# Right halves of the sample's output weights split beside the first outputs; one DRAM tensor for a pair's gated values and one for its sums; attention outputs loaded sooner

## The chip, the core and the metric

The kernel runs on one core of a Trainium2 chip. The metric is the device time of one execution in microseconds (us); the median of three runs before the change is 1537.46 us (1533.11 to 1540.15).

The engines are TensorE (PE, with its weight loads, PEld), VectorE (DVE), ScalarE (ACT), GpSimd (POOL) and SyncE (SP). Each executes its own instructions in order; semaphores order them between engines. In this kernel every DMA is issued by SP, in SP's order, and runs on 16 DMA engines.

## The reference

One encoder layer is applied to two batches with the same weights: the prompt (512 rows) and the sample (1024 rows), each row with 1024 columns, in float32.

```python
def _trunk(x, ...):
    h = _rmsnorm(x, norm_attn_g)
    z = h @ w_in                        # q, k, v, and two halves of a convolution's input
    a_out = _window_attn(q, k, v, bias, band, sink)      # 8 heads, |q-k| <= 128
    c = ca * jax.nn.sigmoid(cb)
    c = _dwconv(c, conv_dw_w, conv_dw_b)                 # 31 taps
    c = jax.nn.silu(_layernorm(c, conv_ln_g, conv_ln_b))
    x = x + jnp.concatenate([a_out, c], axis=-1) @ w_out
    h = _rmsnorm(x, norm_ffn_g)
    u = _dwconv(h @ w_up, ffn_dw_w, ffn_dw_b)            # 3 taps, 2 x 2816 columns
    x = x + (jax.nn.silu(u[..., :D_FF]) * u[..., D_FF:]) @ w_down
    return _rmsnorm(x, norm_final_g)
```

## The kernel before

**Precision and tiles.** Every float32 matrix product is made of three products of parts: an operand is rounded to a high part (fp32r) by a cast on ScalarE, and the low part is the operand less the high part, a subtraction on VectorE or GpSimd. `split` (lines 219 to 224) makes both parts; its low part (L223) goes to GpSimd by default and to VectorE with `dve=True`. Matmuls are 128 x 128 by 128 x 512. The 512 rows of the prompt are blocks 0 to 3, the 1024 rows of the sample blocks 4 to 11, of 128 rows each.

**Slots.** SBUF is cut by hand into slots: 15 of class q (4096 bytes a partition), 4 of class c (4224 bytes), 61 of class h (2048 bytes) and some small ones. `sb.tile` takes the free slot of the least class that is big enough, the one that was freed longest ago first; `among` restricts the classes. A slot is given back when the Python object is dropped, and whoever gets it next waits for the instructions that still use it.

**Order.** The program is written as a main line of matmul steps and generators of side work. Each step calls `tick`, which advances the first generator in the queue `side` at a set rate; `drain` runs a queue to its end. The program's order gives priorities; a scheduler that simulates the time of each instruction then orders each engine's instructions. Only in the stages behind the ones described here is TensorE's order written by hand.

**The stages round the change.**

- The prompt's feed-forward up projection runs over 22 column blocks j (`ffn_step`, L933). For a block, `up_half` multiplies the gate's and the value's columns (L329, L330, L332 in `proj`, into the two banks u), ScalarE evacuates a bank (L888), and VectorE adds the other two taps (L884). `gate` (L906) makes the gated value, 128 x 512, and stores it to the DRAM tensor `gt[j]` (L915). The up weights are split on ScalarE and GpSimd (L222, L223).
- Beside it, as side work, `sample` (L947) runs the sample's attention, loads the attention outputs of blocks 4 and 5 back from `catd` (`load_cat`, L703), loads the output weights `w_out` as 16 halves (8 row chunks kc, each with a left and a right half of 512 columns; `load_wo`, L775), splits all 16 (`split_wo`, on VectorE as `m % 4 < DW2` always holds), and normalises the convolution of blocks 4 and 5 (`conv_norm`, L708). What of it is left behind the last up projection is drained (L973).
- The sample's output projection runs over blocks 4 to 11. `out_half(i, n)` (L746) multiplies block i with half n of the weights: 24 matmuls (L756, L757, L758) into one of three banks u and c, an addition of the input on VectorE (L761), and after the right half a store of the row block to `x1d` and its sum of squares. `scaled` (L1000) scales the block for the next product. Beside it run, as side work, `conv_norm` of the block two ahead and `pair_sums`.
- `conv_norm` loads a block of the convolution from `cvd` (L714), transposes it on TensorE (L720), takes mean and deviation on VectorE (L722, L723) and GpSimd (L206, L207), scales (L726), transposes back (L732), and finishes on ScalarE and VectorE (L735 to L740).
- `pair_sums(p)` (L917) reads the prompt's gated values of blocks 2p and 2p + 1 from DRAM (L920, L921), makes four sums and differences of their left and right halves on GpSimd (L925 to L928), and stores the four, 128 x 256 each, to DRAM tensors `gb[i, p]` (L930). There are 11 pairs. They are read again in the down projection, in `load_next` (L1379, L1383), from about 1155 us on.
- Behind these come the sample's up projection and the down projection of both batches, with TensorE's order by hand.

Of the kernel before, what the change touches and what calls it, by code (L numbers as in the profile page):

```python
# [9 lines left out]
F32 = mybir.dt.float32  # L10
# [3 lines left out]
ALU = mybir.AluOpType  # L14

P = 128
D = 1024
KC = D // P
NT = 512
# [9 lines left out]
NJ = FF // P  # L29
# [21 lines left out]
WOP, WOA, DW, DW2 = 1, 5, 2, 4  # L51
NE = 2
# [116 lines left out]
def tile_hybrid_encoder(ctx: ExitStack, tc: tile.TileContext, xs, rel_bias, norm_attn_g, w_in,  # L169
                        attn_sink, conv_dw_w, conv_dw_b, conv_ln_g, conv_ln_b, w_out, norm_ffn_g,  # L170
                        w_up, ffn_dw_w, ffn_dw_b, w_down, norm_final_g, onehot, outs):
    nc = tc.nc
# [5 lines left out]
    dr = ctx.enter_context(tc.tile_pool(name="dr", bufs=1, space=bass.MemoryType.DRAM))  # L178
# [8 lines left out]
    sb = Slots(lambda tag: homes[tag[0]], dict(q=(15, 4096), c=(4, 4224), h=(61, 2048), d=(2, 2176), s=(32, 64)), "q", KEEP)  # L187
# [14 lines left out]
    warm = cst.tile([P, 1], F32, name="warm")  # L202
    nc.scalar.activation(warm[:], nhalf[:], AF.Exp)

    def rstd_of(ss, n, out):
        nc.gpsimd.tensor_scalar(out, ss, 1.0 / n, EPS, op0=ALU.mult, op1=ALU.add)  # L206
        nc.gpsimd.tensor_tensor(out, out, nhalf[:], op=ALU.pow)  # L207
# [11 lines left out]
    def split(raw, dve=False):  # L219
        shape = list(raw.t.shape[1:])  # L220
        hi, lo = sb.tile(shape, F32R), sb.tile(shape, F32R)
        nc.scalar.copy(hi[:], raw[:])  # L222
        (nc.vector if dve else nc.gpsimd).tensor_tensor(lo[:], raw[:], hi[:].bitcast(F32), op=ALU.subtract)  # L223
        return hi, lo


# [71 lines left out]
    side, pace = deque(), dict(rate=0.0, due=0.0, conv=0.0, credit=0.0, late=0.0)  # L298
# [262 lines left out]
    NB = len(blocks)  # L561
# [141 lines left out]
    def load_cat(i):  # L703
        cats[i, 0] = (sb.tile([4, P], F32R), sb.tile([4, P], F32R))
        for L in range(2):
            nc.sync.dma_start(cats[i, 0][L][:].bitcast(F32), catd[blocks[i][1], :, L, :].rearrange("p (j t) -> p j t", t=P))

    def conv_norm(i):  # L708
        G, b = blocks[i]
        if G["g"] == 0:  # L710
            drain(convs)
        cat = cat_of(i, 1)
        cv = sb.tile([4, P])
        nc.sync.dma_start(cv[:], cvd[G["g"]][:, :, b * P:(b + 1) * P])  # L714
        if G["g"] == 1 and (i, 0) not in cats:
            load_cat(i)
        yield 0.0
        pt = bank("norm")
        for c in range(4):
            nc.tensor.transpose(pt[:, c * P:(c + 1) * P], cv[:, c, :], ident[:])  # L720
        st, mv, rs = sm(6), sm(2), sm(1)
        nc.vector.bn_stats(st[:], pt[:])  # L722
        nc.vector.bn_aggr(mv[:], st[:])  # L723
        rstd_of(mv[:, 1:2], 1.0, rs[:])
        xh = sb.tile([CCH])
        nc.vector.tensor_scalar(xh[:], pt[:], mv[:, 0:1], rs[:], op0=ALU.subtract, op1=ALU.mult)  # L726
        del pt
        for _ in range(YN):
            yield 0.0
        p2 = bank("norm")  # L730
        for c in range(4):
            nc.tensor.transpose(p2[:, c * P:(c + 1) * P], xh[:, c * P:(c + 1) * P], ident[:])  # L732
        y, t = sb.tile([4, P]), sb.tile([4, P])
        for c in range(4):
            nc.scalar.activation(y[:, c, :], p2[:, c * P:(c + 1) * P], AF.Identity,  # L735
                                 scale=lng[:, c:c + 1], bias=lnb[:, c:c + 1])
        nc.scalar.activation(t[:], y[:], AF.Tanh)
        nc.vector.scalar_tensor_tensor(t[:], t[:], 1.0, y[:], op0=ALU.add, op1=ALU.mult)
        nc.scalar.copy(cat[0][:], t[:])
        nc.vector.tensor_tensor(cat[1][:], t[:], cat[0][:].bitcast(F32), op=ALU.subtract)  # L740
        yield 0.0
# [33 lines left out]
    def load_wo(kc, n):  # L775
        raw = wor[kc, n] = sb.tile([NT])
        s = slice(n * NT, (n + 1) * NT)
        if kc < 4:
            for kv in range(NKV):
                r0 = (kv * GRP + kc) * HD  # L780
                nc.sync.dma_start(raw[kv * HD:(kv + 1) * HD, :], w_out[0, r0:r0 + HD, s])
        else:
            nc.sync.dma_start(raw[:], w_out[0, kc * P:(kc + 1) * P, s])

    def split_wo(kc, n, dve=False):
        wo[kc, n] = split(wor.pop((kc, n)), dve)
# [112 lines left out]

    NPAIR = NJ // 2  # L900
    HT = NT // 2
    gt = [dr.tile([P, NT], F32, name=f"gt{j}") for j in range(NJ)]
    gb = {(i, p): dr.tile([P, HT], F32, name=f"gb{i}_{p}") for i in (3, 5, 6, 7) for p in range(NPAIR)}
    HL, HR = slice(0, HT), slice(HT, NT)

    def gate(j, a, b):  # L906
        th, t = bank("gate"), sb.tile([NT])
        nc.scalar.activation(th[:], a[:], AF.Tanh, scale=0.5)
        if j % 4 == VG:
            nc.vector.scalar_tensor_tensor(th[:], th[:], 1.0, a[:], op0=ALU.add, op1=ALU.mult)  # L910
            nc.vector.tensor_tensor(t[:], th[:], b[:], op=ALU.mult)
        else:
            nc.vector.scalar_tensor_tensor(t[:], th[:], 1.0, a[:], op0=ALU.add, op1=ALU.mult)
            nc.gpsimd.tensor_tensor(t[:], t[:], b[:], op=ALU.mult)
        nc.sync.dma_start(gt[j][:], t[:])  # L915

    def pair_sums(p):  # L917

        e, o, x, y = (sb.tile([NT]) for _ in range(4))
        nc.sync.dma_start(e[:], gt[2 * p][:])  # L920
        nc.sync.dma_start(o[:], gt[2 * p + 1][:])  # L921
        yield 0.0
        yield 0.0
        gp = nc.gpsimd.tensor_tensor
        gp(x[:, HR], e[:, HR], o[:, HR], op=ALU.add)  # L925
        gp(x[:, HL], e[:, HL], e[:, HR], op=ALU.subtract)  # L926
        gp(e[:, HR], x[:, HR], e[:, HL], op=ALU.subtract)
        gp(y[:, HL], o[:, HL], e[:, HR], op=ALU.subtract)  # L928
        for i, src in ((5, x[:, HR]), (7, x[:, HL]), (6, e[:, HR]), (3, y[:, HL])):
            nc.sync.dma_start(gb[i, p][:], src)  # L930
        yield 0.0

    def ffn_step(k):  # L933
# [13 lines left out]
    def sample():  # L947
        sink_columns()
        yield from attention(8, 24)
        kt.clear(), vt.clear(), qt.clear(), bias.clear(), score_rows.clear()  # L950
        use.update(norm="a")
        pace.update(rate=RN)
        for m in range(16 + WOA):
            if m in (10, 12):
                load_cat(m // 2 - 1)
            if m < 16:
                load_wo(m // 2, m % 2)
            if m >= WOA:
                split_wo((m - WOA) // 2, m % 2, m % 4 < DW2)
                yield 0.0  # L960
        drain(late)
        for m in range(NE):
            yield from conv_norm(4 + m)

    pace.update(rate=RD, late=CD)
    for k in range(NJ):
# [152 lines left out]
    def out_blocks(i, n):  # L1119
        for _ in out_half(i, n):  # L1120
            tick()
        if n == 1:
            scaled(i)

    side.extend(pair_sums(p) for p in range(NPAIR))
    pace.update(rate=2.2)
    for i in range(4, NB - 2):
        if i + NE < NB:
            side.appendleft(conv_norm(i + NE))
        if i == 8:  # L1130
            pace.update(rate=RE)
            side.appendleft(turned(1, old_bank))
        for n in range(2):
            out_blocks(i, n)
    reserve(4)
    for j in range(2):
        for half in range(2):
# [219 lines left out]
    def load_next(n):  # L1357
        for _ in range(n):
            if ahead:
                key, p = ahead.popleft()  # L1360
                roomy = sum(f[0][0] in "qc" for f in sb.free) > 5
                if (key, p) in second_half:
                    t = second_half.pop((key, p))
                elif key in BRIEF and p % 2 == 0 and p + 1 < NPAIR and roomy:
                    both = sb.tile([2, NT])
                    t, second_half[key, p + 1] = Part(both, 0), Part(both, 1)
                    both = None
                else:
                    t = sb.tile([NT])
                pr[key, p] = t  # L1370
                what, i, n2 = key
                if what == "a":
                    src = ga[i, p][:]
                elif what == "g":
                    n = min(2, NPAIR - 2 * p)
                    for q in range(n):
                        j, h = {1: (0, HL), 2: (1, HL), 4: (1, HR)}.get(i, (0, None))
                        src = gb[i, 2 * p + q][:] if h is None else gt[2 * (2 * p + q) + j][:, h]
                        nc.sync.dma_start(t[:, q * HT:(q + 1) * HT], src)  # L1379
                    continue  # L1380
                else:
                    src = w_down[0, (2 * p + i) * P:(2 * p + i + 1) * P, n2 * NT:(n2 + 1) * NT]
                nc.sync.dma_start(t[:], src)  # L1383
# [239 lines left out]
    u, e, o11, o12 = (acc.pop(n) for n in ("u", "e", "o11", "o12"))  # L1623
# [76 lines left out]
```

## Time and profile before

| | |
|---|---|
| median of 3 runs | 1537.46 us |
| profiled execution | 1537.94 us |
| its span, first to last instruction | 1536.2 us |
| granted TensorE clock, mean | 0.990 |
| VectorE, ScalarE, GpSimd busy | 75%, 52%, 45% |
| moved by DMA | 227.17 MB, mean 148 GB/s |

The profile is of one execution. The span is shorter than the execution's time by 1.7 us, which lie before the first and after the last instruction. Engines' busy times are unions of their instructions' durations; the duration of a matmul overlaps that of the next, so the pace is read from the starts. In rows of instructions `h<-u,fw,h` names what is written and read (q, h, c: slots of those classes; a, b, u, c behind matmuls: PSUM banks; gt, gb, catd, cvd: DRAM tensors); the bracket behind a row is the engine's idle time before it, and who ended it. SPq is SP's queue of DMA issues.

### The profile page before, as it was taken

The numbers are of one execution on the slowest core, as the hardware profiler recorded it, in microseconds if no ns is written. First come the engines' busy times: TensorE is split into PE (matmuls) and PEld (weight loads), VectorE is DVE, ScalarE is ACT, GpSimd is POOL, SyncE is SP. The second block draws the span as 40 slices with busy tenths as digits, with TensorE's granted clock in tenths as the row PEclk, the third lists the DMA queues.
The fourth block names the chain that finished last, engine by engine and source line by source line (L and its number), as shares of the span: only waits on it lengthen the run. The fifth ranks groups of instructions, "written<-read, shape, count | busy, mean of one in ns | idle before, by whom it ended". The sixth has DMA issues, their size and how long they took to land.

```text
span 1536.2 us, 20069 instructions
## 1 busy us (share of the span) xinstructions
PE 1491.5 (97%) x6843; PEld 1229.2 (80%) x6843; DVE 1151.5 (75%) x1624; ACT 795.7 (52%) x1404; POOL 694.5 (45%) x546
## 2 busy tenths in 40 slices
PE   8898899999999999899999999999999999999998
PEld 6787787788888888687777888888888788888886
DVE  6998777678788795854777777777776855668884
ACT  4635655435777786623454555555545633343354
POOL 6651342436667776637433555555545000003345
PEclk9999999999999999999999999999999999999999
DMA  6563324637344335769422333333331772356654
GB/s 226 165 190 92 96 84 115 199 115 236 110 127 136 121 124 179 228 220 314 151 74 72 100 103 103 103 103 103 103 125 60 237 269 77 118 163 215 212 180 165
DMA packets 228780, 227.17 MB, mean 148 GB/s; under 512 B 13268, under 2 KB 168348, under 8 KB 228549
## 3 DMA queue, kind: packets, MB, share of 16 engines
q1 hardware_dynamic: 228677, 225.88, 45.8%
q8 instruction: 54, 0.88, 0.2%
q14 instruction: 49, 0.40, 0.1%
HBM read 164.74 MB, written 62.14 MB: 148 GB/s over the span
## 4 chain that ended last, share of the span: by engine, by line
PE 49%; DMA 3%; POOL 2%; DVE 1%; ACT 1%; issue 1%; SPq 1%; POOLq 0%; ACTq 0%; DVEq 0%
PE w L1113 8%; PE w L1111 8%; PE w L1112 8%; PE w L1445 7%; PE w L1446 7%; PE w L1447 7%; DMA h<-gt 1%; POOL h L926 0%; PE u L329 0%; PE u L756 0%; PE u L330 0%; PE u L332 0%; PE u L758 0%; PE u L757 0%; DMA gt<-h 0%
## 5 line engine op out<-in xcount | busy, mean ns | idle before, releaser
L223 POOL TENSOR_TENSOR q<-q,q 128x1024 fp32r<-128x1024 f32 x72 | 175.1, 2437 | 115.6 <-ACT q L222 43.5
L987 POOL TENSOR_TENSOR q<-q,q 128x512 fp32r<-128x512 f32 x101 | 140.4, 1397 | 153.5 <-ACT q L1097 141.4
L987 DVE TENSOR_TENSOR h<-h,h 128x512 fp32r<-128x512 f32 (+2 forms) x202 | 154.0, 795 | 65.5 <-ACT h L991 25.5
L1447 PE MATMUL w<-h,h 128*128 128x512 f32 x462 | 179.7, 389 | 0.0
L1445 PE MATMUL w<-h,h 128*128 128x512 f32 x458 | 178.2, 389 | 1.3 <-DVE q L1232 1.3
L1446 PE MATMUL w<-h,h 128*128 128x512 f32 x458 | 178.2, 389 | 0.0
L1113 PE MATMUL w<-h,q 128*128 128x512 f32 x448 | 174.4, 389 | 1.1 <-POOL q L987 1.1
L1111 PE MATMUL w<-h,q 128*128 128x512 f32 x448 | 174.8, 390 | 0.4 <-ACT w L1185 0.4
L329 PE MATMUL u<-h,q 128*128 128x512 f32 x400 | 161.4, 404 | 5.0 <-DVE h L884 4.0
L1112 PE MATMUL w<-h,q 128*128 128x512 f32 x426 | 165.8, 389 | 0.0
L330 PE MATMUL u<-h,q 128*128 128x512 f32 x400 | 158.8, 397 | 0.0
L332 PE MATMUL u<-h,q 128*128 128x512 f32 x384 | 151.1, 394 | 1.2 <-POOL q L223 1.2
L384 DVE SCALAR_TENSOR_TENSOR c<-c,cvw,c 128x512 f32<-128x512 f32 x184 | 138.0, 750 | 2.7
L984 POOL TENSOR_TENSOR q<-q,q 128x1024 f32<-128x1024 f32 x12 | 33.2, 2780 | 230.8 <-DVE q L984 212.7
L991 ACT CAST h<-h 128x512 fp32r<-128x512 f32 x120 | 71.7, 620 | 96.5 <-DVE h L987 44.2
L329 PE MATMUL b<-h,q 128*128 128x512 f32 x256 | 103.4, 404 | 3.9 <-DVE d L414 2.2
L330 PE MATMUL b<-h,q 128*128 128x512 f32 x256 | 102.2, 399 | 0.0
L1445 PEld LDWEIGHTS w<-h,h 128*128 128x128 f32 x458 | 86.0, 188 | 19.7 <-issue 1.7
L332 PE MATMUL b<-h,q 128*128 128x512 f32 x256 | 101.7, 398 | 0.0
L1447 PEld LDWEIGHTS w<-h,h 128*128 128x128 f32 x462 | 86.7, 188 | 17.9
L222 ACT CAST q<-q 128x1024 fp32r<-128x1024 f32 (+1 forms) x73 | 75.9, 1044 | 47.5 <-POOL q L223 16.9
L1446 PEld LDWEIGHTS w<-h,h 128*128 128x128 f32 x458 | 86.0, 188 | 17.7
(432 smaller groups left out, 3669.4 us busy)
## 6 DMA issues: line engine op xcount, KB each, us to landing
q<-in_w_up SPq DMA_DIRECT2D x88, 512.0 KB
ga<-q SPq DMA_DIRECT2D x64, 256.0 KB
h<-ga SPq DMA_DIRECT2D x57, 256.0 KB
q<-in_w_in SPq DMA_DIRECT2D x28, 512.0 KB
h<-in_w_down SPq DMA_DIRECT2D x52, 256.0 KB
q<-in_x_sample SPq DMA_DIRECT2D x15, 512.0 KB
x1d<-q SPq DMA_DIRECT2D x11, 512.0 KB
gt<-h SPq DMA_DIRECT2D x22, 256.0 KB
```

The costliest lines, as they stand in the source:

```text
L223: (nc.vector if dve else nc.gpsimd).tensor_tensor(lo[:], raw[:], hi[:].bitcast(F32), op=ALU.subtract)
L329: nc.tensor.matmul(out, whi[:, kc, :], hi[:], start=(kc == 0), stop=False)
L330: nc.tensor.matmul(out, whi[:, kc, :], lo[:], start=False, stop=False)
L332: nc.tensor.matmul(out, wlo[:, kc, :], hi[:], start=False, stop=(kc == KC - 1))
L384: nc.vector.scalar_tensor_tensor(acc[:], src(t), w(t), acc[:], op0=ALU.mult, op1=ALU.add)
L987: (eng or nc.vector).tensor_tensor(out, a, b, op=ALU.subtract)
L1111: nc.tensor.matmul(out, whi[:, s], hi[:], start=(start and c == 0), stop=False, **go)
L1112: nc.tensor.matmul(out, whi[:, s], lo[:], start=False, stop=False, **go)
L1113: nc.tensor.matmul(out, wlo[:, s], hi[:], start=False, stop=(stop and c == 3), **go)
L1445: nc.tensor.matmul(out, sh[:, c], th[:], start=(p == 0), stop=False)
L1446: nc.tensor.matmul(out, sh[:, c], tl[:], start=False, stop=False)
L1447: nc.tensor.matmul(out, sl[:, c], th[:], start=False, stop=(p == NPAIR - 1))
```

## The change

- **Output weights.** In `sample`, only the eight left halves are loaded and split before the normalisations of blocks 4 and 5; the eight right halves are loaded behind them, and split by a new generator `right_halves` at the head of the side queue of the output projection, on VectorE as before.
- **Attention outputs.** `load_cat` of blocks 4 and 5 is called after two and four loads of half weights, in place of ten and twelve.
- **Order of outputs.** The first outputs are (4, left), (5, left), (4, right), (5, right), in place of both halves of block 4 and then both of block 5. The normalisation of block 6 stands in the side queue behind the right halves.
- **Pairs.** A pair's two gated values lie in one DRAM tensor `gt[p]`, and its four sums in one, `gb[p]`. `pair_sums` reads the first with one DMA into a slot of class c, writes the sums to another slot of class c, and stores them with one DMA. The values are the same. The first sum is ordered on GpSimd behind the last low part that `split` has put there (`ended["lo"]`, `tc.issue_after`). The down projection's reads follow the new tensors.

```diff
+    ended = {}
...
         nc.scalar.copy(hi[:], raw[:])
-        (nc.vector if dve else nc.gpsimd).tensor_tensor(lo[:], raw[:], hi[:].bitcast(F32), op=ALU.subtract)
+        ins = (nc.vector if dve else nc.gpsimd).tensor_tensor(lo[:], raw[:], hi[:].bitcast(F32), op=ALU.subtract)
+        if not dve:
+            ended["lo"] = ins.ins
         return hi, lo
...
-    gt = [dr.tile([P, NT], F32, name=f"gt{j}") for j in range(NJ)]
-    gb = {(i, p): dr.tile([P, HT], F32, name=f"gb{i}_{p}") for i in (3, 5, 6, 7) for p in range(NPAIR)}
+    gt = [dr.tile([P, 2, NT], F32, name=f"gt{p}") for p in range(NPAIR)]
+    gb = [dr.tile([P, 4, HT], F32, name=f"gb{p}") for p in range(NPAIR)]
+    GB = {5: 0, 7: 1, 6: 2, 3: 3}
...
-        nc.sync.dma_start(gt[j][:], t[:])
+        nc.sync.dma_start(gt[j // 2][:, j % 2, :], t[:])
 
     def pair_sums(p):
 
-        e, o, x, y = (sb.tile([NT]) for _ in range(4))
-        nc.sync.dma_start(e[:], gt[2 * p][:])
-        nc.sync.dma_start(o[:], gt[2 * p + 1][:])
+        g, r = sb.tile([2, NT], among="c"), sb.tile([4, HT], among="c")
+        nc.sync.dma_start(g[:], gt[p][:])
         yield 0.0
         yield 0.0
         gp = nc.gpsimd.tensor_tensor
-        gp(x[:, HR], e[:, HR], o[:, HR], op=ALU.add)
-        gp(x[:, HL], e[:, HL], e[:, HR], op=ALU.subtract)
-        gp(e[:, HR], x[:, HR], e[:, HL], op=ALU.subtract)
-        gp(y[:, HL], o[:, HL], e[:, HR], op=ALU.subtract)
-        for i, src in ((5, x[:, HR]), (7, x[:, HL]), (6, e[:, HR]), (3, y[:, HL])):
-            nc.sync.dma_start(gb[i, p][:], src)
+        e, o = g[:, 0, :], g[:, 1, :]
+        with tc.issue_after(ended["lo"]):
+            gp(r[:, 0, :], e[:, HR], o[:, HR], op=ALU.add)
+        gp(r[:, 1, :], e[:, HL], e[:, HR], op=ALU.subtract)
+        gp(r[:, 2, :], r[:, 0, :], e[:, HL], op=ALU.subtract)
+        gp(r[:, 3, :], o[:, HL], r[:, 2, :], op=ALU.subtract)
+        nc.sync.dma_start(gb[p][:], r[:])
         yield 0.0
...
-        for m in range(16 + WOA):
-            if m in (10, 12):
-                load_cat(m // 2 - 1)
-            if m < 16:
-                load_wo(m // 2, m % 2)
+        for m in range(KC + WOA):
+            if m in (2, 4):
+                load_cat(m // 2 + 3)
+            if m < KC:
+                load_wo(m, 0)
             if m >= WOA:
-                split_wo((m - WOA) // 2, m % 2, m % 4 < DW2)
+                split_wo(m - WOA, 0, True)
                 yield 0.0
         drain(late)
         for m in range(NE):
             yield from conv_norm(4 + m)
+        for kc in range(KC):
+            load_wo(kc, 1)
...
+    def right_halves():
+        for kc in range(KC):
+            split_wo(kc, 1, True)
+            yield 0.0
+
+    side.extend((right_halves(), conv_norm(4 + NE)))
     side.extend(pair_sums(p) for p in range(NPAIR))
     pace.update(rate=2.2)
     for i in range(4, NB - 2):
-        if i + NE < NB:
+        if 4 < i < NB - NE:
             side.appendleft(conv_norm(i + NE))
...
-        for n in range(2):
-            out_blocks(i, n)
+        for k, n in {4: ((4, 0), (5, 0), (4, 1)), 5: ((5, 1),)}.get(i, ((i, 0), (i, 1))):
+            out_blocks(k, n)
...
-                        src = gb[i, 2 * p + q][:] if h is None else gt[2 * (2 * p + q) + j][:, h]
+                        src = gb[2 * p + q][:, GB[i], :] if h is None else gt[2 * p + q][:, j, h]
```

## The prediction

> **What bounds the kernel now.** The page first: one number says which engine to follow.
>
> ```profile
> PE 1491.5 (97%) x6843; PEld 1229.2 (80%) x6843; DVE 1151.5 (75%) x1624; ACT 795.7 (52%) x1404; POOL 694.5 (45%) x546
> ```
>
> TensorE is busy for 1491.5 us of a span of 1536.2, and the change neither adds nor removes a matmul. So it can only win back time in which TensorE idles or runs slowly, at most in the stretches that it touches. The second view is therefore the table by windows round the end of the first half's feed-forward loop and the output projection of the sample. Its columns are the window's length and the busy time of PE, PEld, DVE, ACT and POOL, then the granted clock, the DMA share and GB/s.
>
> ```profile
> 590.00:640.00 50.00, 49.90 (x246) 41.44 (x244) 33.83 (x56) 35.13 (x67) 28.83 (x16) 1.00 0.70 221
> 640.00:656.00 16.00, 10.18 (x36) 7.39 (x35) 15.11 (x13) 6.92 (x11) 10.62 (x5) 0.79 0.67 211
> 656.00:690.00 34.00, 34.00 (x160) 28.04 (x160) 17.97 (x29) 8.13 (x14) 12.22 (x19) 1.00 0.65 208
> 690.00:740.00 50.00, 47.83 (x225) 38.15 (x224) 21.74 (x30) 19.51 (x41) 36.21 (x49) 1.00 0.89 296
> 740.00:756.00 16.00, 13.86 (x63) 11.45 (x62) 11.15 (x20) 3.44 (x7) 5.13 (x9) 0.89 0.48 165
> ```
>
> Two short stretches lose time: 640 to 656 (5.8 us idle, clock 0.79) and 740 to 756 (2.1 us idle, clock 0.89). Between them 690 to 740 loses 2.2. The third view is the timeline of TensorE inside them; the bracket is the idle time before the row and who ended it.
>
> ```profile
> 645.04 0.50 PE L756 MATMUL c<-h,h 128*128 128x512 f32 x1 [0.34 <-DMA h<-catd]
> ...
> 647.27 0.50 PE L758 MATMUL c<-h,h 128*128 128x512 f32 x1 [1.50 <-DMA h<-catd]
> ...
> 652.67 0.76 PE L329 MATMUL u<-h,q 128*128 128x512 f32 x1 [3.97 <-DVE h L884]
> ...
> 656.19 0.40 PE L332 MATMUL u<-h,q 128*128 128x512 f32 x1
> 656.42 0.39 PE L329 MATMUL u<-h,q 128*128 128x512 f32 x1
> ...
> 726.85 0.63 PE L732 MATMUL a<-ident,h 128*128 128x128 f32 x4 [1.44 <-DVE h L726]
> ...
> 740.38 1.04 PE L1034 MATMUL b<-ident,q 128*128 128x128 f32 x8
> 741.17 0.48 PE L756 MATMUL c<-h,h 128*128 128x512 f32 x1
> ...
> 745.04 1.76 PE L720 MATMUL a<-ident,h 128*128 128x128 f32 x7 [2.14 <-DMA h<-cvd]
> 746.45 0.78 PE L756 MATMUL u<-h,h 128*128 128x512 f32 x1
> ...
> 748.31 0.40 PE L757 MATMUL u<-h,h 128*128 128x512 f32 x1
> ```
>
> **First stall.** The waits are 0.34 + 1.50 + 3.97 = 5.81 us. After the last of them eight matmuls take from 652.67 to 656.19, 3.52 us, where the pace just after is 0.23 each (656.19 to 656.42), 1.84 for eight: 1.68 more go to the lowered clock. Together **7.5 us**. **Second stall.** The wait is 2.14; then seven transposes and four matmuls take from 745.04 to 748.31, 3.27 us. At full pace a transpose is 0.10 (eight from 740.38 to 741.17), so 0.70 + 0.92 = 1.62: 1.65 lost, **3.8 us** in all. The wait of 1.44 at 726.85 shows no slow matmuls behind it. These 12.7 us are nearly all there is to win here.
>
> Who causes the first stall is in the timeline of VectorE, and of GpSimd beside it.
>
> ```profile
> 638.75 10.76 DVE L223 TENSOR_TENSOR h<-h,h 128x512 fp32r<-128x512 f32 x5
> 649.54 0.69 DVE L685 TENSOR_TENSOR h<-b,h 64x512 f32<-64x512 f32 x1
> 650.26 0.69 DVE L223 TENSOR_TENSOR h<-h,h 128x512 fp32r<-128x512 f32 x1
> 650.99 1.53 DVE L884 SCALAR_TENSOR_TENSOR h<-u,fw,h 128x511 f32<-128x511 f32 x2
> ...
> 657.41 2.68 DVE L223 TENSOR_TENSOR h<-h,h 128x512 fp32r<-128x512 f32 x4 [0.72 <-ACT h L222]
> ```
>
> ```profile
> 640.63 8.33 POOL L223 TENSOR_TENSOR q<-q,q 128x1024 fp32r<-128x1024 f32 x3
> ```
>
> Five splits of output weights take 10.76 us, 2.15 each, while GpSimd does its own splits of up weights from 640.63 to 648.96; four of the same shape with GpSimd idle take 2.68, 0.67 each. The taps (L884) that empty the up projection's bank stand behind the five on VectorE, so TensorE waits until 652.67.
>
> **The change part by part.** *Right halves out of the way.* Before, all 16 halves are split ahead of the first output.
>
> ```profile
> L223 DVE TENSOR_TENSOR h<-h,h 128x512 fp32r<-128x512 f32 x16 | 23.0, 1467 | 2.5 <-ACT h L222 1.8 <-POOL h L914 0.6
> ```
>
> That row (groups from 600 to 850) is the 16 splits: 23.0 us, 1.47 each. Eight are now made after the last up projection in the program's order, so 8 x 1.47 = 11.8 us leave VectorE ahead of the taps. To end a wait of 3.97 two of the five splits in the run suffice, and what is next late is only TensorE's own work: it is dense from 656 to 690. I take the whole 3.97 and 1.68 as gone. The bounds are 0 (the other eight still fall into GpSimd's splits) and all of it. The same 11.8 us come back later at most: 656 to 690 has 34.00 - 17.97 = 16.0 us of idle VectorE, and the casts on ScalarE (8.13 busy of 34) fit too. If that cover is gone, rival B gives the price. Eight loads (twelve issues on SP) move with them, from ahead of the normalisations of blocks 4 and 5 to behind them.
>
> *Attention outputs sooner.* The loads from `catd` stand behind ten half loads, now behind two; 1.50 + 0.34 us of wait go with them. They read tensors that were written long before, so nothing new is waited for. Cost: two weight halves land later by 1 MB of `catd` at 211 GB/s, 5 us, which lies beside the last feed-forward matmuls; 0.
>
> *Order (4,0), (5,0), (4,1), (5,1).* The same 96 matmuls. Left halves first give 48 x 0.23 = 11.0 us of work before a right half is needed. Block 4's residual is scaled one half output (5.5 us) later; its reader is the turning at block 8, far off: 0.
>
> *One tensor for a pair.* These rows are the pair sums on GpSimd (groups from 660 to 745), the DMA issues on SP, and pieces of the chain of waits with their lengths.
>
> ```profile
> L925 POOL TENSOR_TENSOR h<-h,h 128x256 f32<-128x256 f32 x11 | 9.4, 854 | 14.8 <-DMA h<-gt 14.8
> L926 POOL TENSOR_TENSOR h<-h 128x256 f32<-128x256 f32 x11 | 9.1, 828 | 0.0
> L927 POOL TENSOR_TENSOR h<-h,h 128x256 f32<-128x256 f32 x11 | 8.6, 779 | 0.7
> L928 POOL TENSOR_TENSOR h<-h,h 128x256 f32<-128x256 f32 x11 | 8.5, 774 | 5.8 <-DVE h L738 5.4
> ```
>
> ```profile
> L930 SPq DMA_DIRECT2D gb<-h x44: 319/382/1394, 681.1 to 742.3; - x44
> ```
>
> ```profile
> 675.04 3.31 DMA h<-gt
> ...
> 715.72 7.02 DMA h<-gt
> ...
> 725.51 3.67 DMA gb<-h
> ...
> 740.59 0.38 SPq L706
> 741.06 0.41 SPq L930
> 741.65 3.35 DMA h<-cvd
> ```
>
> The arithmetic is unchanged, four instructions a pair, 0.854 + 0.828 + 0.779 + 0.774 = 3.2 us. Issues fall from 22 loads and 44 stores to 11 and 11: 44 x 0.382 = 16.8 us less on SP's queue, which is no bound by itself, but the second stall is a load of `cvd` issued at 741.65 behind the stores of the last pairs, landing 3.35 later. The bytes stay. What is new is a limit: a pair takes two of only four c slots, so two pairs are in flight, where before they drew on 61 h slots. A pair's trip is load (3.31 to 7.02), sums 3.2, store 3.67: 10.2 to 13.9 us, so 5.1 to 7.0 a pair and 56 to 76 us for eleven. Now they take from 678.5 to 742.1, 63.6. But the c slots are free early, and GpSimd is nearly idle ahead of them:
>
> ```profile
> 667.52 0.19 POOL L206 TENSOR_SCALAR s<-s 128x1 f32<-128x1 f32 x1 [15.43 <-DVE s L723]
> ...
> 678.51 1.16 POOL L925 TENSOR_TENSOR h<-h,h 128x256 f32<-128x256 f32 x1 [8.89 <-DMA h<-gt]
> ```
>
> So I expect the sums to start some 20 us sooner, to spread the traffic that now fills the DMA engines (0.89 from 690 to 740), and to be over before the last `cvd` load: the second stall goes, -3.8. Bounds: 0 and 3.8. The wait on the last weight split, which the first sum gets, costs 0: GpSimd ended its splits at 648.96, 29 us before the first sum of now.
>
> *What is new and not shown by any row* is a late operand among the moved things: a right half, or a normalisation behind a sum on GpSimd. Its bounds are 0 and one more first stall with its slow clock, 3.97 + 1.68 = 5.6; I take two of the small kind that stand here already, 1.50 + 1.44 = 2.9, since the cover is 11 us and more.
>
> The two meet in a rule. The Trainium skill, "SBUF — State Buffer", section "SBUF: two separate sides", says that VectorE and GpSimd share one port pair as an exclusive lock held for a whole instruction; the rows agree in kind (2.15 against 0.67 us). By it the moved splits would pay again beside the pair sums, but one sum of 0.8 us each and not one split of 2.8, so 8 x 0.8 = 6.4 us, inside VectorE's 16.0; where they aren't inside, it is rival B.
>
> **The sum.** -7.5 - 3.8 + 2.9 = -8.4 us. The profiled execution is 1537.94 (span 1536.2 and 1.7 round it), 0.5 above the median of 1537.46; the same difference from the median gives **1529.1**.
>
> **The rivals.** *A: the second stall only moves.* The pairs' new limit keeps stores in front of loads of `cvd` or `catd`. For it: 5.1 to 7.0 us a pair is no faster than now. Against it: the early start and 44 issues fewer. -7.5 + 2.9 = -4.6: 1532.9.
>
> *B: the right halves come late.* If their 2 MB start to load only with output (4,0), then at 211 GB/s and 3.3 us to land they are there after 13 us, and eight splits at 2.15 end after 3.3 + 17.2 = 20.5. The last is needed after 11.0 + 5.5 = 16.5: 4.0 us, and the slow clock's 1.7, come back as a new wait before L756. Against it: SP and VectorE have room from 656 on. With the second stall kept: -7.5 + 5.7 = -1.8, 1535.7. The lock that the skill's page on SBUF names would be its cause.
>
> *C: it doesn't do what it says*: the moved splits, being ready, still go in front of the taps. Then only the `catd` wait goes: 1537.46 - 1.8 = 1535.7, also within.
>
> *D: slower, by the c slots.* GpSimd takes instructions in order. A sum that writes a slot must wait for the store of the pair two before (3.67 us), and behind it on GpSimd stand the two small instructions of a normalisation's deviation, for which VectorE's L726 and then TensorE's transposes L732 wait, as they do at 726.85 for 1.44. One such hold is 3.67, with a slow clock of 1.65 after it 5.3. It decides from three of the six remaining blocks on: 3 x 5.3 = 16.0 - 7.5 = +8.5, 1546.0. Against it: normalisations lead by two blocks, some 22 us of matmuls.
>
> **How the numbers follow.** Forecast 0.52 with a range of its own from 1524.7 (no new loss, and the 1.44 gone too) to 1531.8 (new loss 5.6); A 0.20; B 0.10; C 0.04; D 0.14. A measurement of this kernel tells about 0.5% from no change, 7.7 us: faster means below 1529.8. Three quarters of the forecast's range lie there (0.39) and some 0.06 of A: 0.45. Slower is D, 0.14. The rest is 0.41. The range runs from 1524.0, just under the forecast's own low, to 1540.0, which leaves out most of D and a little below.
>
> **What would show it.** Right: L329 after the attention's last instructions without a wait over 1 us and the clock at 1.00 from 640 to 660; eight splits at L223 on VectorE before the last taps and eight after; pair sums from about 655; no wait for `cvd` over 1 us. Wrong: a wait of L756 to L758 on VectorE's splits or the loads of weights (B), of L732 with GpSimd's sums or a store of `gb` in front (D), or losses after 756, where nothing is meant to change.

## The result, and the profile after

The changed kernel takes 1525.82 us (median of five runs, 1523.73 to 1528.78). The kernel before, run beside it, has a median of 1534.06 over five runs, its first three among them. The ratio is 0.9935, with a 95% interval of 0.9916 to 0.9955. Taken from 1534.06 that is 10.0 us (6.9 to 12.9); the medians differ by 8.2. The forecast was 8.4 us less, on a median of 1537.46 that later runs of the kernel before brought down. The time lies inside the range and below the 1529.8 that was set for faster. It is 3.3 us under the forecast of 1529.1, while the median of the kernel before came down by 3.4: the difference was forecast well, the level was too high.

The profiled execution of the kernel after took 1528.78 us, with a span of 1527.0. The table by windows over the same stretches as before (length; busy PE, PEld, DVE, ACT, POOL; clock; DMA share; GB/s):

```profile
590.00:640.00 50.00, 50.00 (x251) 41.95 (x250) 29.75 (x54) 35.23 (x65) 28.96 (x17) 1.00 0.72 221
640.00:656.00 16.00, 14.84 (x67) 11.90 (x66) 13.70 (x17) 5.64 (x9) 15.42 (x14) 1.00 0.72 239
656.00:690.00 34.00, 31.39 (x144) 25.06 (x143) 19.28 (x27) 11.78 (x23) 19.52 (x22) 1.00 0.88 313
690.00:740.00 50.00, 49.20 (x239) 40.17 (x238) 30.24 (x41) 20.64 (x42) 25.86 (x39) 1.00 0.70 243
740.00:756.00 16.00, 16.00 (x80) 13.29 (x79) 13.05 (x19) 7.26 (x16) 5.25 (x7) 1.00 0.18 64
```

Both stretches with a lowered clock are back at 1.00: 640 to 656 idles for 1.2 us (5.8 before), 740 to 756 not at all. In 656 to 690, which was dense, TensorE now idles for 2.6 us, and the DMA share there is 0.88 where it was 0.65. These are the rows of TensorE's timeline with a wait of over 0.5 us in front:

```profile
647.76 0.47 PE L333 MATMUL u<-h,q 128*128 128x512 f32 x1 [1.16 <-DVE h L888]
...
682.05 0.50 PE L760 MATMUL c<-h,h 128*128 128x512 f32 x1 [0.87 <-DVE q L765]
...
687.28 0.66 PE L724 MATMUL a<-ident,h 128*128 128x128 f32 x4 [1.50 <-DMA h<-cvd]
```

No matmul runs slowly behind any of them. (Line numbers move by 2 to 14: L225 is the low part of a split, L333, L334, L336 the up projection, L724 a normalisation's transposes, L760 to L762 an output, L765 the addition of the input, L888 the taps.) The two groups that the argument turned on, on VectorE and on SP's queue, and the pair sums, in rows of their timelines:

```profile
639.76 2.88 DVE L225 TENSOR_TENSOR h<-h,h 128x512 fp32r<-128x512 f32 x1 [1.46 <-POOL h L919]
...
643.40 2.05 DVE L225 TENSOR_TENSOR h<-h,h 128x512 fp32r<-128x512 f32 x1
...
663.18 1.82 DVE L225 TENSOR_TENSOR h<-h,h 128x512 fp32r<-128x512 f32 x2
...
679.86 0.88 DVE L225 TENSOR_TENSOR h<-h,h 128x512 fp32r<-128x512 f32 x1 [3.16 <-DMA gt<-h]
...
681.32 0.67 DVE L765 TENSOR_TENSOR q<-c,q 128x512 f32<-128x512 f32 x1
681.92 0.68 DVE L225 TENSOR_TENSOR h<-h,h 128x512 fp32r<-128x512 f32 x1
```

```profile
647.64 1.43 POOL L931 TENSOR_TENSOR c<-c 128x256 f32<-128x256 f32 x2
...
663.47 0.99 POOL L931 TENSOR_TENSOR c<-c 128x256 f32<-128x256 f32 x1 [7.63 <-DMA c<-gt]
```

```profile
680.31 0.56 SPq L718 DMA_DIRECT2D h<-cvd  x1
...
711.76 0.32 SPq L935 DMA_DIRECT2D gb<-c  x1
...
718.43 0.52 SPq L718 DMA_DIRECT2D h<-cvd  x1
```

The left halves' last splits still stand beside GpSimd's and take 2 to 3 us, but there are two of them where there were five. The sums start at 647.64, right behind the last weight split, and the last pair is stored at 711.76 (before: 742.3). The last `cvd` load leaves at 718.43; before, it left at 741.65.

The wait of 0.87 us at 682.05 is a price of the right halves. The addition that TensorE waits for there (681.32) stands on VectorE behind a right half's split, and that split waited 3.16 us, until 679.86, for the store of a gated value.

To compare kernels by stage, TensorE's lost time is added up from the starts of its rows: each distance from one row to the next, less 0.227 us for a 512 column matmul and 0.099 for a 128 column one. It counts waits and slow clock together.

| lost, us | 605-640 | 640-660 | 660-690 | 690-740 | 740-760 | 760-790 | 605 to 790 |
|---|---|---|---|---|---|---|---|
| before | 1.0 | 8.3 | 0.4 | 3.9 | 4.2 | 1.0 | 18.8 |
| after | 0.6 | 1.6 | 3.6 | 2.2 | 0.4 | 1.8 | 10.2 |

8.6 of the 9.2 us between the two profiled executions come from this stretch.

### The profile page after: what moved, and what is told of

Its sections match the earlier page's. It is cut to its first block, busy times and chain, and to the rows that moved or that the text cites. A ratio compares the mean times of both kernels' runs of the same rounds, so it can differ in the third digit from the quotient of the medians.

```text
span 1527.0 us, 19962 instructions
## 1 busy us (share of the span) xinstructions
PE 1487.8 (97%) x6843; PEld 1227.8 (80%) x6843; DVE 1150.5 (75%) x1624; ACT 795.4 (52%) x1404; POOL 691.2 (45%) x546
## 4 chain that ended last, share of the span: by engine, by line
PE 88%; DMA 3%; DVE 3%; POOL 2%; ACT 2%; issue 1%; SPq 0%; POOLq 0%; DVEq 0%; ACTq 0%
PE w L1120 9%; PE w L1118 9%; PE w L1119 9%; PE w L1458 7%; PE w L1459 7%; PE w L1460 7%; PE u L333 6%; PE u L334 6%; PE u L336 6%; PE b L333 3%; PE b L336 3%; PE b L334 3%; PE u L761 2%; PE u L762 2%; PE u L760 2%; PE a L665 1%
## 5 line engine op out<-in xcount | busy, mean ns | idle before, releaser
L225 POOL TENSOR_TENSOR q<-q,q 128x1024 fp32r<-128x1024 f32 x72 | 174.4, 2428 | 117.2 <-ACT q L224 44.2
L994 DVE TENSOR_TENSOR h<-h,h 128x512 fp32r<-128x512 f32 (+2 forms) x202 | 157.7, 813 | 66.7 <-ACT h L998 26.5
L333 PE MATMUL u<-h,q 128*128 128x512 f32 x400 | 159.9, 400 | 2.0 <-DVE h L888 1.2
L334 PE MATMUL u<-h,q 128*128 128x512 f32 x400 | 157.2, 393 | 0.0
L336 PE MATMUL u<-h,q 128*128 128x512 f32 x384 | 150.7, 392 | 0.9 <-POOL q L225 0.9
L333 PE MATMUL b<-h,q 128*128 128x512 f32 x256 | 104.1, 407 | 5.7 <-DVE d L418 3.5
L334 PE MATMUL b<-h,q 128*128 128x512 f32 x256 | 102.5, 401 | 0.0
L336 PE MATMUL b<-h,q 128*128 128x512 f32 x256 | 102.2, 400 | 0.0
```

What stands on the lines that cost most here:

```text
L225: ins = (nc.vector if dve else nc.gpsimd).tensor_tensor(lo[:], raw[:], hi[:].bitcast(F32), op=ALU.subtract)
L333: nc.tensor.matmul(out, whi[:, kc, :], hi[:], start=(kc == 0), stop=False)
L334: nc.tensor.matmul(out, whi[:, kc, :], lo[:], start=False, stop=False)
L336: nc.tensor.matmul(out, wlo[:, kc, :], hi[:], start=False, stop=(kc == KC - 1))
L994: (eng or nc.vector).tensor_tensor(out, a, b, op=ALU.subtract)
```

## The experiments

Two theories stood against the one on record. Theory 1 is the prediction's: two stalls with two causes, the splits of the weights and the late `cvd` load behind the pairs. Theory 2 gives everything to the weights, theory 3 to the pairs. All runs but one were timed in five rounds against the kernel before, on the same chip; the runs come from three chips, so ratios are compared and not times. "Lost" is the sum from 605 to 790 us, as above, from each run's profile; "last load" is the issue of the last `cvd` load, counted from the sample's last score matmul (614.3 us in the profile before, 609.0 to 614.5 in the others).

| run | ratio to before, 95% | lost, us | last load, us |
|---|---|---|---|
| before | 1 | 18.8 | 127.4 |
| after, first profile | 0.9935, 0.9916 to 0.9955 | 10.2 | 103.9 |
| e8_after, after once more | 0.9940, 0.9918 to 0.9961 | 11.3 | 105.0 |
| e1_weights | 1.0003, 0.9988 to 1.0019 | 17.7 | 119.7 |
| e2_pairs | 0.9958, 0.9941 to 0.9974 | 12.8 | 106.2 |
| e3_cat | 0.9986, 0.9976 to 0.9997 | 16.6 | 123.7 |
| e4_many | 0.9974, 0.9962 to 0.9985 | 17.2 | 111.5 |
| e5_late | 0.9932, 0.9907 to 0.9956 | 9.7 | 100.7 |
| e6_stores | 0.9962, 0.9949 to 0.9976 | 16.7 | 110.7 |
| e7_swap | 0.9940, 0.9916 to 0.9964 | 13.8 | 107.5 |
| e9_small | 0.9950, 0.9932 to 0.9967 | 10.5 | 103.3 |
| e11_ahead | 0.9966, 0.9951 to 0.9981 | 13.3 | 104.0 |
| e12_free | 0.9957, 0.9941 to 0.9974 | 13.2 | 106.4 |

**The kernel after, once more (e8_after).**

> The kernel after, unchanged, once more beside the others on the same chip: 0.9916 to 0.9955 of before. Its profile tells how much of a stage's time differs between executions of one program; the lost time between 605 and 790 should be within 1 us of the first profile's 10.2.

Lost time came out 1.1 us apart, a little over what was expected. From this one pair I take 2 us as about the least difference in that column that one profile can show.

**The weights alone (e1_weights).** The edit is the kernel after with `gt`, `gb`, `pair_sums` and their reads as before:

```diff
-        g, r = sb.tile([2, NT], among="c"), sb.tile([4, HT], among="c")
-        nc.sync.dma_start(g[:], gt[p][:])
+        e, o, x, y = (sb.tile([NT]) for _ in range(4))
+        nc.sync.dma_start(e[:], gt[2 * p][:])
+        nc.sync.dma_start(o[:], gt[2 * p + 1][:])
...
-        nc.sync.dma_start(gb[p][:], r[:])
+        for i, src in ((5, x[:, HR]), (7, x[:, HL]), (6, e[:, HR]), (3, y[:, HL])):
+            nc.sync.dma_start(gb[i, p][:], src)
```

> The weights, the attention loads and the order of outputs as after the change, the pairs as before it. Theory 1 (two stalls, two causes): the first stall's 7.5 us go, the second stall's 3.8 stay, with some 1 to 3 us of new small waits: 4.5 to 6.5 us faster than before, ratio 0.9958 to 0.9971; TensorE waits for a load of cvd or behind sums between 690 and 760. Theory 2 (the weights alone carry everything, the second stall was a follower of the first): 8 to 10 us faster, 0.9935 to 0.9948. Theory 3 (the pairs' traffic carries it): within 1.5 us of before, 0.999 to 1.001.

Measured: no difference at all, which none but theory 3 had. Yet the first stall went. These are three rows of the table by windows, and three waits from TensorE's timeline:

```profile
640.00:656.00 16.00, 15.20 (x72) 12.21 (x71) 11.98 (x19) 6.88 (x14) 6.98 (x7) 1.00 0.74 227
...
690.00:740.00 50.00, 45.24 (x212) 36.19 (x211) 24.70 (x35) 14.92 (x31) 31.59 (x47) 0.97 0.90 292
...
756.00:785.00 29.00, 26.62 (x119) 20.68 (x118) 23.83 (x33) 12.20 (x23) 11.79 (x11) 0.94 0.29 91
```

```profile
696.91 0.66 PE L724 MATMUL a<-ident,h 128*128 128x128 f32 x4 [2.29 <-DMA h<-cvd]
...
732.88 0.50 PE L762 MATMUL u<-h,h 128*128 128x512 f32 x1 [1.54 <-DMA h<-catd]
...
760.75 0.66 PE L1040 MATMUL b<-ident,q 128*128 128x128 f32 x4 [0.90 <-DVE h L993]
```

From 640 to 660 only 1.3 us are lost, 7.0 less than before; from 690 to 790, 15.2 us, 6.1 more than before. TensorE reached the outputs earlier and waited there, for loads of `cvd` and `catd` and for VectorE, with a lowered clock behind. The won time was given back within the same stage.

**The pairs alone (e2_pairs).** The kernel before with the new `gt`, `gb` and `pair_sums` and the order of the first sum.

> The pairs as after the change (one tensor each, class c slots, the first sum behind the last weight split), the weights, attention loads and order as before it. Theory 1: the wait of the up projection for VectorE's taps near 650 stays at 3 to 5 us with its slow clock, pair sums run from about 650 to 715, the wait for cvd near 745 goes: 2 to 4 us faster, 0.9974 to 0.9987. Theory 2: no difference, 0.999 to 1.001. Theory 3: 8 us or more faster, 0.995 or less.

Measured: 0.9958, 6.4 us, between theory 1 and theory 3. The wait for the taps stayed (4.0 us of the table of waits), as theory 1 had it, and the waits for `cvd` went. The lost time fell from 8.3 to 5.7 in 640 to 660 and from 9.1 to 5.2 in 690 to 790; in the first of the two the waits for `catd` went as well, though their loads weren't moved.

**The attention loads alone (e3_cat).**

```diff
-            if m in (10, 12):
-                load_cat(m // 2 - 1)
+            if m in (2, 4):
+                load_cat(m // 2 + 3)
```

> The kernel before with one edit: the attention outputs of blocks 4 and 5 are loaded after two and four half loads of weights, all 16 halves as before. Theory 1: the waits for catd at 645 and 647 (1.84 us) go, the wait for VectorE's taps stays or takes them over, since the splits still stand in front of the taps: 0 to 2 us faster, 0.9987 to 1.000. Rival: the catd waits were what let the clock drop and the taps come late, and all of the first stall goes: 5 to 7.5 us faster, 0.995 to 0.997.

Measured: 0.9986, at the edge of theory 1's range. The waits for `catd` are gone and the taps still hold TensorE for 2.7 us.

**As many DMAs as before (e4_many).** The kernel after with

```diff
-        nc.sync.dma_start(g[:], gt[p][:])
+        for q in range(2):
+            nc.sync.dma_start(g[:, q, :], gt[p][:, q, :])
...
-        nc.sync.dma_start(gb[p][:], r[:])
+        for q in range(4):
+            nc.sync.dma_start(gb[p][:, q, :], r[:, q, :])
```

> The kernel after, with two loads and four stores a pair in place of one and one (22 and 44 DMAs as before the change), in the same tensors and the same class c slots. If the early start in free slots is what ends the second stall: as the kernel after, within 1.5 us (0.993 to 0.9955 of before), sums from about 648. If the 44 issues fewer on SP or the bigger packets are what ends it: the wait for cvd comes back and 2 to 4 us are lost to the kernel after, 0.9955 to 0.998 of before.

Measured: 0.9974, with 4.74 us of wait for `cvd` at 685. The early start was there (its first stores leave before 660), and most of the gain was not. The wait near 745 did not come back: 740 to 760 loses 0.3 us.

**A late start (e5_late).** The kernel after, each pair's load behind the store of the last gated value:

```diff
-        nc.sync.dma_start(gt[j // 2][:, j % 2, :], t[:])
+        ended["gt"] = nc.sync.dma_start(gt[j // 2][:, j % 2, :], t[:]).ins
...
-        nc.sync.dma_start(g[:], gt[p][:])
+        with tc.issue_after(ended["gt"]):
+            nc.sync.dma_start(g[:], gt[p][:])
```

> The kernel after, with the pairs' loads ordered on SP behind the store of the last gated value, so that pair sums start near 690 in place of 648; as few and as big DMAs as after. If the early start of the sums is what the pairs' part is worth: the waits for loads of cvd and catd between 690 and 760 come back and about 6 us of the gain are lost, 0.997 to 1.000 of before. If the fewer DMAs are what it is worth: within 1.5 us of the kernel after, 0.993 to 0.9955.

Measured: 0.9932, the same as the kernel after. In SP's timeline the sums' stores end as late as in the kernel before, and still the `cvd` loads aren't late:

```profile
669.98 0.56 SPq L718 DMA_DIRECT2D h<-cvd  x1
...
714.60 0.52 SPq L718 DMA_DIRECT2D h<-cvd  x1
...
740.05 0.32 SPq L936 DMA_DIRECT2D gb<-c  x1
```

So the early start isn't needed to end the second stall, nor for the gain. It moves the losses, though. From 660 to 690 this run loses 0.3 us, where the kernel after loses 3.6; from 740 to 760 it loses 3.4, in two waits of outputs for the casts of late normalisations (L743, 1.7 and 0.9 us), where the kernel after loses 0.4.

**The stores alone split (e6_stores), and small packets in one DMA (e9_small).** The first is the kernel after with the four stores of e4_many alone. The second keeps one store, but lays the four sums out apart:

```diff
-    gb = [dr.tile([P, 4, HT], F32, name=f"gb{p}") for p in range(NPAIR)]
+    gb = [dr.tile([4, P, HT], F32, name=f"gb{p}") for p in range(NPAIR)]
...
-        nc.sync.dma_start(gb[p][:], r[:])
+        nc.sync.dma_start(gb[p][:].rearrange("q p t -> p q t"), r[:])
```

> The kernel after with one load and four stores a pair: 33 DMAs more, where the run with two loads and four stores has 44 more. If the stores on SP's queue in front of the loads of cvd are what cost that run its 4 us: most of it is lost here too, 0.9955 to 0.998 of before, with a wait of TensorE for cvd of 2 us or more between 660 and 715. If the split loads cost it: as the kernel after, 0.993 to 0.9955.

> The kernel after with the four sums of a pair laid out apart in DRAM (4 x 128 x 256 in place of 128 x 4 x 256), still stored by one DMA: one issue on SP, but packets of 1 KB as in the run with four stores. If the number of issues on SP in front of the loads of cvd is what the split stores cost: as the kernel after, 0.992 to 0.9955 of before, no wait for cvd over 2 us. If the smaller packets on the DMA engines are: as the run with four stores, 0.995 to 0.9976, with a wait for cvd of 3 us or more near 685.

Measured: 33 stores more give 0.9962, near the whole split's 0.9974; the same pieces of 1 KB in one DMA give 0.9950. The intervals of these two ratios overlap; the profiles tell them apart: 16.7 us lost, with 7.6 us of waits for `cvd`, against 10.5 us with 0.5 of such waits. The rows show where the time of e6_stores goes: first SP's queue of e6_stores ahead of the `cvd` load at 679.11, then TensorE waiting for it and the slow clock behind.

```profile
671.88 2.52 SPq L936 DMA_DIRECT2D gb<-c  x4
674.48 0.56 SPq L718 DMA_DIRECT2D h<-cvd  x1
675.14 0.60 SPq L710 DMA_DIRECT2D h<-catd  x1
675.84 1.35 SPq L936 DMA_DIRECT2D gb<-c  x3
...
679.11 0.56 SPq L718 DMA_DIRECT2D h<-cvd  x1
```

```profile
686.92 1.11 PE L724 MATMUL a<-ident,h 128*128 128x128 f32 x4 [6.05 <-DMA h<-cvd]
687.68 0.77 PE L762 MATMUL u<-h,h 128*128 128x512 f32 x1
688.26 0.63 PE L760 MATMUL u<-h,h 128*128 128x512 f32 x1
```

Counted from the last score matmul, that load leaves at 679.11 - 609.0 = 70.1 us, and in the kernel after at 680.31 - 614.5 = 65.8. It takes 7 to 8 us to land in both; what differs is when it is issued. By these profiles what counts is that the stores are split into more DMAs, and not their packets. Why was not told apart. It can be SP's own time for an issue, or the DMAs' places in the queues behind SP. It can also be SP's order: the scheduler puts 18 stores, of four and a half pairs, ahead of the first `cvd` load of e6_stores (674.48), and 4, of four pairs, ahead of that of the kernel after (673.83), and SP stands for 2.8 us in front of the four at 671.88, waiting for a sum.

**GpSimd's splits beside VectorE's (e10_dve).** One run of the kernel before with

```diff
-            upw[k, half] = split(upr.pop((k, half)))
+            upw[k, half] = split(upr.pop((k, half)), k >= NJ - 2)
```

> The kernel before with the low parts of the last two column blocks' up weights (four splits, 128 x 1024) made on VectorE in place of GpSimd, so that GpSimd has no split beside the output weights' splits at 638 to 650. If GpSimd's splits are what stretches VectorE's (2.15 us against 0.67): all output weight splits after 630 take 0.67 to 0.75 us but those beside another GpSimd instruction, and the wait for VectorE's taps near 652 shrinks to 0 to 2.5 us though VectorE has four splits of some 1.3 us more. Rival (the casts or the weights' loads set their pace, or SBUF traffic stretches them): some still take 2 us or more with GpSimd idle.

This is VectorE's timeline, then GpSimd's:

```profile
636.28 3.00 DVE L223 TENSOR_TENSOR h<-h,h 128x512 fp32r<-128x512 f32 x3
639.20 3.48 DVE L223 TENSOR_TENSOR q<-q,q 128x1024 fp32r<-128x1024 f32 x3
...
643.43 2.36 DVE L223 TENSOR_TENSOR h<-h,h 128x512 fp32r<-128x512 f32 x2
...
652.63 0.68 DVE L223 TENSOR_TENSOR h<-h,h 128x512 fp32r<-128x512 f32 x1
```

```profile
636.50 1.61 POOL L914 TENSOR_TENSOR h<-h,h 128x512 f32<-128x512 f32 x1 [2.75 <-DVE h L884]
643.55 1.70 POOL L687 TENSOR_TENSOR h<-h,h 64x512 fp32r<-64x512 f32 x1 [5.43 <-DVE h L685]
```

Every output weight split from 636 on that stands beside no GpSimd instruction takes 0.67 to 0.69 us; the rows beside one average 1.0 and 1.2. That GpSimd's instructions stretch VectorE's splits is shown. What this does to TensorE's wait at 652 isn't: in front of the taps TensorE now waits 3.57 us for `catd`, at 646, and that can hide what it would have waited for them. Counted from the last score matmul, the taps end 2.3 us sooner than in the kernel before, though VectorE has four splits more ahead of them. The time of that one run (1540.24) is no gain, and more was lost at the outputs.

**Without the order on GpSimd (e12_free).** The kernel after without `tc.issue_after(ended["lo"])`.

> The kernel after without the order of the first sum behind the last weight split on GpSimd. Pairs 0 and 1 are loaded near 398, so their first sums can run there too, and no later pair before its gated values. If the order protects GpSimd's up weight splits: TensorE waits for a split in the up projection, 1 to 4 us slower than the kernel after, 0.9945 to 0.998 of before. If nothing hung on it: within 1 us of the kernel after, 0.9925 to 0.9955.

Measured: 0.9957, inside the range given for an order that protects something, but its interval meets that of the kernel after, so the ratio alone doesn't settle it. The profile points the same way: 13.2 us lost against 10.2 and 11.3, with a wait of 3.90 us for the taps at 647 again and a clock of 0.79 from 640 to 656. TensorE did not wait for an up weight split, as had been expected, but for VectorE.

**Two tries to beat it.** e7_swap puts block 6's normalisation ahead of the right halves; e11_ahead loads `cvd` for blocks 6 and 7 ahead of the right halves:

```diff
-    side.extend((right_halves(), conv_norm(4 + NE)))
+    side.extend((conv_norm(4 + NE), right_halves()))
```

```diff
+        for i in range(4 + NE, 6 + NE):
+            ready[i] = load_cv(i)
         for kc in range(KC):
             load_wo(kc, 1)
```

> The kernel after with block 6's normalisation put ahead of the right halves in the side queue, so that its load of cvd is issued sooner; meant to beat the kernel after. If the load's late issue is what TensorE waits for at 687 (1.50 us): that wait goes, 0 to 2 us faster than the kernel after, 0.992 to 0.9940 of before. Rival: the right halves come later by it, and a wait of the third output (4, right) takes its place: 0.9935 to 0.9955.

> The kernel after with the cvd loads of blocks 6 and 7 issued ahead of the loads of the right halves; meant to beat the kernel after. If their place behind the pairs' transfers is what costs the 3.6 us between 660 and 690: the wait of TensorE for cvd at 687 goes and 1 to 3 us with it, 0.991 to 0.9935 of before. Rival: another operand is late right behind it (right halves, the sums on GpSimd): as the kernel after, 0.9925 to 0.9955.

Neither is faster than the kernel after, and e11_ahead lies above both of its ranges. In both the wait for `cvd` at 687 went, and waits for a normalisation's scaling on VectorE took its place (L736 for L730, 2.5 us, in e7_swap; L743 for L737, 3.6 us, in e11_ahead). No version that was run beats the kernel after beyond the intervals.

## Why the prediction was right, and where its reasons were not

**What bounds the kernel: right.** 8.6 of the 9.2 us between the two profiled executions lie between 605 and 790 us.

**The terms, by place: right.** The first stall was to give 7.5; 640 to 660 lost 6.7 less. The second was to give 3.8; 740 to 760 lost 3.8 less. The new losses were to be 2.9; the other stretches from 605 to 790 lost 8.2 in place of 6.3, 1.9 more. The sum of the three was -8.4 and the table's is -8.6, closer than one profile can show. Two of the signs named for right failed by little: the waits at 647.76 and 687.28 are 1.16 and 1.50 us, where none over 1 was to be. And six of the eight right halves are split ahead of the last taps (682.52), where all were to come behind them.

**The cause of the first stall: right.** e10_dve shows GpSimd's instructions stretching VectorE's splits. e1_weights shows that eight splits less ahead of the taps, with the `catd` loads sooner, cut the wait for them from 3.97 to 0.8 us; the `catd` loads alone (e3_cat) leave 2.7. The clock came back with it, as the slow matmuls' row had it.

**What each part is worth: wrong.** The sum gave the weights 7.5 of the gain, as if what stands behind were ready. Done alone they end their stall and bring nothing (1.0003), since the outputs then start sooner and wait for `cvd` and `catd`. The pairs, down for 3.8, bring 6.4 alone. The step that failed is "what is next late is only TensorE's own work: it is dense from 656 to 690". The stage was dense because TensorE had come late to it. That the total came out although neither part's worth did is in part luck: the sum has no term for what one part does to the other.

**How the second stall goes: wrong in its mechanism.** "So I expect the sums to start some 20 us sooner ... and to be over before the last `cvd` load" came true (647.64, 711.76), but isn't the cause of the gain: e5_late stores its last pair at 740 and has the same time. What the prediction had set aside in the words "16.8 us less on SP's queue, which is no bound by itself" was the lever: with 33 stores more the lost time goes from 10.2 to 16.7 us, and with the same bytes in small packets in one DMA it stays at 10.5. Among the runs that differ in the pairs alone, those with few DMAs lose 9.7 to 11.3 us, with early or late sums; with many DMAs e4_many (early) loses 17.2 and e1_weights (late, with the pairs' old tensors and slots) 17.7. What ended the wait at 745 itself stays open. It is gone with few late DMAs (e5_late), with many early ones (e4_many and e6_stores lose 0.3 and 0.4 us from 740 to 760, and their loss stands near 685), and even in e1_weights, whose pairs are as before: there TensorE waits for other loads.

**Costs taken as nothing: right in size, but not nothing.** The right halves' casts held an output for 0.35 us in the first profile after and for 1.2 in the second, and a split held the addition before another output, 0.87 and 1.40 us. Their splits beside the pair sums cost little: the eight from 663 on add up to 6.0 us, 0.76 each, against 0.67 alone; the estimate by the lock that the Trainium skill's "SBUF — State Buffer" describes ("SBUF: two separate sides") was 6.4 us more, and 0.7 was measured. Only four of the eight stood beside a pair sum. Rival B left no wait of its size. Rival A's condition (a load of `cvd` late behind the pairs) is what remains, 1.50 us at 687.

Rival D left a small trace. These rows of the kernel after are from VectorE, GpSimd and TensorE:

```profile
689.03 0.18 DVE L727 BATCH_NORM_AGGREGATE s<-s 128x2 f32<-128x6 f32 x1
```

```profile
691.27 0.74 POOL L931 TENSOR_TENSOR c<-c 128x256 f32<-128x256 f32 x1 [2.29 <-DMA c<-gt]
...
693.48 0.19 POOL L208 TENSOR_SCALAR s<-s 128x1 f32<-128x1 f32 x1
```

```profile
695.99 0.63 PE L736 MATMUL a<-ident,h 128*128 128x128 f32 x4 [0.46 <-DVE h L730]
```

The deviation (L208) could have run behind 689.2, but stands on GpSimd behind a sum that waited for its load until 691.27, and TensorE waited 0.46 us in the end. The sum waits for a load, where D had it wait for a store. In e7_swap the same path costs 2.5 us: the sum waits until 677.77, and the deviation runs at 679.99.

## What to carry to other kernels

Before a stall's length is booked as gain, look at what the freed engine meets next: loads that come just in time for an engine that is late come too late for one that is early, and two changes that are each worth little or half may only pay together. Where one queue issues all DMAs, splitting transfers ahead of a small load that the bounding engine waits for can cost time, though the queue has room on average, as here; joining pieces into one DMA is cheap to try. And a part's worth is known by running it alone, not by the place where the time came back.

## What the runs showed of the hardware that had not been expected

An issue of a DMA on SP is not always short. In e4_many, a row of SP's queue, in a stretch (656 to 690) where the DMA engines were at 0.92:

```profile
685.15 4.30 SPq L718 DMA_DIRECT2D h<-cvd  x1
```

Issues of the same line take 0.56 us at 676.11 and 680.40 in that run; the next issue on SP came at 689.55, behind it. Packets of 1 KB in place of 4 KB, in DMAs of the same size and number, showed no cost in the time (0.9950 against 0.9935 and 0.9940, the intervals overlapping), though the DMA share from 656 to 690 rose from 0.88 to 0.95.
